# Hybrid decoder trunk on one core: weight tiles at another byte offset with each load, three buffers in place of four, two strips ahead

## The chip, the cores and the metric

The kernel runs on one core of a Trainium2 chip. The metric is the device time of one launch in microseconds (us). The times of before are three runs of the same program; the profile is of one more execution.

## What is computed

A batch of one, 512 tokens, 1024 channels. Two layers follow each other, each in a "macaron" form: half a SwiGLU feed-forward, a mixer, half a SwiGLU feed-forward. The first layer's mixer is an mLSTM in chunks; then one shared set of keys and values is made from the residual stream, and the second layer's mixer is a sparse attention over it (compressed blocks, selected blocks, a window). Cut to what matters here:

```python
D_MODEL, SEQ, D_FF = 1024, 512, 2816

def swiglu(h, w_in, w_out):
    a, b = jnp.split(h @ w_in, 2, axis=-1)
    return (jax.nn.silu(a) * b) @ w_out

x = x + 0.5 * swiglu(rmsnorm(x, g), w_in, w_out)    # ffn0
x = x + mlstm_mixer(rmsnorm(x, g), ...)             # mlstm
x = x + 0.5 * swiglu(rmsnorm(x, g), w_in, w_out)    # ffn1
...                                                 # kv: shared keys and values
x = x + 0.5 * swiglu(rmsnorm(x, g), w_in, w_out)    # ffn2
x = x + nsa_mixer(rmsnorm(x, g), ...)               # nsa
x = x + 0.5 * swiglu(rmsnorm(x, g), w_in, w_out)    # ffn3
```

All in float32. The four feed-forwards hold most of the multiplications.

## The kernel before

**Numbers.** Each float32 operand is split in two parts of the matmul's type: a high half (names ending in hi) and the low rest (lo). A product is three matmuls, hi·hi, hi·lo and lo·hi (`mm3`), issued by the helper at L234. The weights are the stationary operand, 128 x 128 at a time, and the activations the moving one: tiles of 128 channels by 512 tokens, or halves of them with 256 columns. Activations are named x (a feed-forward's normed input), t (sums of halves of x, 256 columns) and g (the gated hidden units).

**Stages.** In order of time: ffn0, mlstm, ffn1, kv, ffn2 (woven with the compression of keys and values), nsa, ffn3. ffn0, ffn1 and ffn3 (`SEVEN`) form their input products by a scheme with seven products in place of eight for a 2 x 2 split (`by_seven`); ffn2 does so from its second block on. The hidden units are worked through in blocks (`EVENS`: 0 to 8, 8 to 16 and 16 to 22, in units of 128; `LATER` in ffn2). A block is a row of by_seven units, one for a and one for b of each pair of hidden tiles, and then the block's share of the output product, `ffn_out`, eight strips with 512 columns.

**A unit** of `by_seven` has seven products of 12 matmuls with 256 columns (four channel tiles by three). VectorE takes the results out of PSUM between them: fq (L492) after the third product, fw (L495) and fu (L497) after the fourth, fw (L502) after the sixth, fu (L507) after the seventh. ScalarE copies the first (L487). A unit needs seven sums of weight quarters ("forms") in four groups, each in one pair of weight tiles: a11 and s1, s2 and s3, s4 and a12, and a22 alone. The quarters q come by DMA (`fetch`, L176), VectorE makes the sums s (`add_quarters`, L198 to L201), and `load_forms` splits each form: ScalarE writes the high half (L243), VectorE the low half as the difference (L244).

**Loads.** A "strip" in what follows is one such pair of tiles whi and wlo, 128 x 1024, from the pool "w" with four buffers. Other weights (ffn_out, the projections) come by `load_weight`: a DMA on SyncE's queue into wraw (two buffers), ScalarE writes whi (L171), VectorE wlo (L172). What is loaded when is set by a list: a dry pass records each `weight()` and `plan()` in the order that they are asked for, and in the real pass `weight()` issues entries of that list until 1 + `ahead` strips are ready, the one asked for among them. So the code of a load is issued `ahead` strips before its use, and stands at that place in the queues of SyncE, ScalarE and VectorE. Entries "fetch" and "add" stand in the list too and are issued with the strip behind them. `ahead` is 3 in ffn0, ffn1 and ffn3, 2 in ffn2 until its second block, then 3; from the fifth output strip of a feed-forward's last block on it is 2, as in the mixers. Within an engine, work runs in the order issued; a tile's next use waits until the last reader of the buffer is done.

```python
while self.order and len(self.ready) < 1 + self.ahead:
    self.load_weight()
key, w = self.ready.popleft()
```

**Places.** `STEP` and `placed` (L400 to L408) give the tiles t and g of ffn0, ffn1 and ffn3 64 words more than they need and start each at another multiple of 16 bytes in them (ffn3's t in steps of 4 words by a table of its own). x, the weights, and t and g of ffn2 start at the beginning of their tiles.

Of the kernel before, what the change touches and what calls it, by code (L numbers as in the profile page):

```python
# [11 lines left out]
F32R = mybir.dt.float32r  # L12
# [7 lines left out]
P = 128  # L20
# [58 lines left out]
class Steps:  # L79


    def __init__(self, gen):
        self.gen, self.may, self.due = gen, next(gen), 0.0
# [25 lines left out]
class Net:  # L109
    def __init__(self, ctx, tc, a, order=None):  # L110
        self.tc, self.nc, self.a, self.ctx = tc, tc.nc, a, ctx
        pool = lambda name, **k: ctx.enter_context(tc.tile_pool(name=name, **k))
        self.const = pool("const", bufs=1)
        self.hp = pool("h", bufs=1)
        self.wp = pool("w", bufs=4)
        self.xp = pool("x", bufs=8)
        self.sp = pool("stat", bufs=1)
        self.order = None if order is None else deque(order)
        self.asked = []
        self.ready = deque()  # L120
        self.raws, self.sums = {}, {}
        self.fp = None
        self.compressed = False
        self.ahead = 2


    def load_first(self):


        nc = self.nc  # L130
        name, idx = self.order.popleft()
        ap = self.a[name][idx]
        raw = self.wp.tile([P, 1024], F32, name="wraw", tag="wraw", bufs=2)
        hi = self.wp.tile([P, 1024], F32R, name="whi", tag="whi")
        lo = self.wp.tile([P, 1024], F32R, name="wlo", tag="wlo")
        v = lambda t: t.rearrange("p (n m) -> p n m", m=P)
        a, b = slice(0, 512), slice(512, 1024)
        for c, k in (a, slice(0, 4)), (b, slice(4, 8)):
            nc.scalar.dma_start(v(raw)[:, k], ap[:, k])
        nc.vector.tensor_copy(hi[:, a], raw[:, a])  # L140
        nc.vector.tensor_tensor(lo[:, a], raw[:, a], hi[:, a].bitcast(F32), op=ALU.subtract)
        self.ready.append(((name, idx), (v(hi), v(lo))))
        self.rest = lambda: self.split(raw[:, b], hi[:, b], lo[:, b])

    def load_weight(self):
        nc = self.nc
        name, idx = self.order.popleft()
        if name == "fetch":
            return self.fetch(*idx)
        if name == "add":  # L150
            return self.add_quarters(*idx)
        if name == "form":
            self.ready.append(((name, idx), self.load_forms(*idx)))
            return
        ap = self.a[name][idx] if idx else self.a[name]
        o = 1
        if len(ap.shape) == 4:
            p, o, n, m = ap.shape
        else:
            p, n, m = ap.shape  # L160
        w = o * n * m
        raw = self.wp.tile([P, 1024], F32, name="wraw", tag="wraw", bufs=2)
        if o == 1:
            nc.sync.dma_start(raw[:p, :w].rearrange("p (n m) -> p n m", m=m), ap)
        else:
            nc.sync.dma_start(raw[:p, :w].rearrange("p (o n m) -> p o n m", o=o, m=m), ap)
        hi = self.wp.tile([P, 1024], F32R, name="whi", tag="whi")
        lo = self.wp.tile([P, 1024], F32R, name="wlo", tag="wlo")

        for c in (slice(0, w // 2), slice(w // 2, w)) if name[0] in "mkc" else (slice(0, w),):  # L170
            nc.scalar.activation(hi[:p, c], raw[:p, c], AF.Copy)  # L171
            nc.vector.tensor_tensor(lo[:p, c], raw[:p, c], hi[:p, c].bitcast(F32), op=ALU.subtract)  # L172
        v = lambda t: t[:p, :w].rearrange("p (n m) -> p n m", m=m)
        self.ready.append(((name, idx), (v(hi), v(lo))))
# [28 lines left out]
    def load_forms(self, i, p, group):  # L203

        q, s = self.raws[i, p], self.sums[i, p]
        forms = ((q[1, 1], s[1]), (s[2], s[3]), (s[4], q[1, 2]), (q[2, 2],))[group]
        hi = self.wp.tile([P, 1024], F32R, name="whi", tag="whi")
        lo = self.wp.tile([P, 1024], F32R, name="wlo", tag="wlo")
        out = []
        for j, f in enumerate(forms):  # L210
            c = slice(512 * j, 512 * j + 512)
            self.split(f, hi[:, c], lo[:, c])
            out.append(tuple(t[:, c].rearrange("p (n m) -> p n m", m=P) for t in (hi, lo)))
        return out
# [159 lines left out]
    def ffn(self, i, given=None):  # L374

        nc, tc = self.nc, self.tc
        seven, r = i in SEVEN, None
        self.qbufs = 2 if seven else 1
        self.ahead = 3 if seven else 2
        TT, STT = nc.vector.tensor_tensor, nc.vector.scalar_tensor_tensor  # L380
        N = T // 2
        with ExitStack() as ctx:
# [4 lines left out]
            def room(name, words=96):  # L387

                nonlocal gp
                inner.close()  # L390
                gp = self.fp = inner.enter_context(tc.tile_pool(name=name, bufs=8, reuse_waits="tile"))

                nc.vector.memset(gp.tile([P, words], F32, name="home", tag="home", bufs=1)[:, :1], 0.0)
# [151 lines left out]
            for k0, k1 in EVENS if seven else LATER:  # L545
                gs, fold = [], seven and k1 < FB
                if not seven and k0 == LATER[1][0]:
                    brief.close()
                    room("fg2b", 32)
                    self.ahead = 3  # L550
                for p in range(k0, k1, 2) if seven or k0 else range(k0, k1):
                    if p and (seven or k0):
                        if p in units:
                            ts = [silu(t) for t in (yield from by_seven(p))]
                        else:
                            ts = []
                            for j in range(2):
                                w = self.weight("ffn_in", i, p + j)
# [903 lines left out]
```

## Time and profile before

| what | value |
|---|---|
| median of 3 runs | 1975.43 us (1973.61 to 1975.85) |
| profiled execution, its time | 1974.49 us |
| profiled execution, its span | 1972.7 us |
| matmuls, line L234, 256 columns on t | 3 x 1184 |
| matmuls, 256 columns on x | 3 x 888 |
| matmuls, 512 columns on g | 3 x 704 |
| matmuls, 512 columns on x | 3 x 480 |
| DMA, HBM read | 177.10 MB, 91 GB/s over the span |

The span is the time from the first to the last instruction of the profiled execution; the run's own time has 1.8 us more around it. PE is TensorE's matmuls, PEld its loading of weights, DVE VectorE, ACT ScalarE, SP SyncE, POOL GpSimd. Matmuls are pipelined: two neighbours overlap in the records, so a matmul's mean duration is longer than the distance from one start to the next, and a change of the one shows in the other. "<-" behind an idle time names what ended it. Times of a timeline count from the span's start. ffn0 runs until about 342 us, mlstm to 575, ffn1 to 912, kv to 1024, ffn2 to 1350, nsa to 1600, ffn3 to the end.

### The profile page before, as it was taken

What the parts mean: (1) busy time and instruction counts of PE and PEld (TensorE: products, weight loads), DVE (VectorE), ACT (ScalarE), POOL (GpSimd) and SP (SyncE); (2) the same over time, 40 slices, a digit from 0 to 9 for tenths busy, and PEclk for the clock granted to TensorE, in tenths of its full rate; (3) what the DMA queues carried; (4) which work ended last, traced back from release to release, by engine and by line L of the source; (5) the groups of instructions that cost most, each with busy time, mean ns of one, the idle gap of its engine ahead of it and who ended that gap; (6) DMA issues with size and microseconds to landing.
All of it is one profiled execution on the core that took longest, in us unless ns stands there. A gap on an engine that the chain in (4) does not pass through costs nothing.

```text
span 1972.7 us, 31765 instructions
## 1 busy us (share of the span) xinstructions
PE 1951.8 (99%) x11946; PEld 1724.3 (87%) x11946; DVE 1610.1 (82%) x3128; ACT 1014.6 (51%) x1912; POOL 167.4 (8%) x218
## 2 busy tenths in 40 slices
PE   9999999999999999999999999999999999999999
PEld 7989899788879999898788989898777879999897
DVE  8969879767888879698677979696788988879695
ACT  6525345455655435245354435354889965435242
POOL 0000000012200000000100000001444410000000
PEclk9999999999999999999999999999999999999999
DMA  5333422323232423323433333313232122323322
GB/s 190 109 100 102 117 77 74 111 86 97 65 118 86 118 85 98 106 72 105 114 121 119 114 111 97 104 63 116 74 88 65 54 97 86 118 82 101 106 72 91
DMA packets 81818, 192.80 MB, mean 98 GB/s; under 512 B 9856, under 2 KB 10752, under 8 KB 81664
## 3 DMA queue, kind: packets, MB, share of 16 engines
q1 hardware_dynamic: 80272, 188.02, 31.5%
q8 instruction: 94, 1.54, 0.3%
q0 software_dynamic: 384, 1.05, 0.3%
q10 hardware_dynamic: 1008, 1.70, 0.2%
q14 instruction: 60, 0.49, 0.1%
HBM read 177.10 MB, written 2.10 MB: 91 GB/s over the span
## 4 chain that ended last, share of the span: by engine, by line
PE 83%; DVE 8%; ACT 3%; DMA 2%; issue 1%; POOL 1%; SPq 0%; DVEq 0%; ACTq 0%; POOLq 0%
PE pmm L234 75%; PE vps L234 2%; PE S L234 1%; ACT pr L1202 1%; DVE wlo L172 1%; PE po L234 1%; DVE wlo L244 1%; DMA q<-in_ffn_in 1%; PE paux L234 1%; PE pt L1233 1%; DVE pr L1199 1%; PE pn L234 1%; ACT whi L171 1%; DVE ptl L244 0%; DMA wraw<-in_ffn_in 0%
## 5 line engine op out<-in xcount | busy, mean ns | idle before, releaser
L234 PE MATMUL pmm<-xhi,whi 128*128 128x256 f32 (+1 forms) x1376 | 444.2, 323 | 1.0 <-ACT whi L171 0.5
L234 PE MATMUL pmm<-xhi,wlo 128*128 128x256 f32 (+1 forms) x1376 | 442.5, 322 | 0.7 <-DVE wlo L172 0.7
L234 PE MATMUL pmm<-xlo,whi 128*128 128x256 f32 (+1 forms) x1376 | 442.2, 322 | 0.9 <-DVE xlo L288 0.8
L171 ACT ACTIVATE whi<-wraw 128x512 fp32r<-128x512 f32 (+3 forms) x258 | 203.9, 810 | 317.0 <-PE pmm L234 202.8
L234 PE MATMUL pmm<-thi,wlo 128*128 128x256 f32 x1184 | 333.0, 282 | 1.0 <-DVE wlo L244 1.0
L234 PE MATMUL pmm<-tlo,whi 128*128 128x256 f32 x1184 | 332.7, 281 | 0.0
L234 PE MATMUL pmm<-thi,whi 128*128 128x256 f32 x1184 | 332.4, 281 | 0.0
L234 PEld LDWEIGHTS pmm<-xhi,wlo 128*128 128x128 f32 x1376 | 260.5, 189 | 20.4 <-DVE wlo L172 1.1
L234 PEld LDWEIGHTS pmm<-xlo,whi 128*128 128x128 f32 x1376 | 260.6, 189 | 20.1 <-DVE xlo L288 2.7
L234 PE MATMUL pmm<-glo,whi 128*128 128x512 f32 x704 | 276.6, 393 | 0.8 <-DVE glo L244 0.8
L234 PEld LDWEIGHTS pmm<-xhi,whi 128*128 128x128 f32 x1376 | 260.3, 189 | 19.3 <-ACT whi L171 0.9
L234 PE MATMUL pmm<-ghi,wlo 128*128 128x512 f32 x704 | 276.8, 393 | 0.0
L234 PE MATMUL pmm<-ghi,whi 128*128 128x512 f32 x704 | 274.7, 393 | 0.0
L172 DVE TENSOR_TENSOR wlo<-wraw,whi 128x512 fp32r<-128x512 f32 (+3 forms) x258 | 237.9, 933 | 44.2 <-ACT whi L171 42.2
L243 ACT ACTIVATE whi<-s 128x512 fp32r<-128x512 f32 x222 | 139.5, 628 | 248.0 <-PE pmm L234 139.8
L234 PEld LDWEIGHTS pmm<-thi,wlo 128*128 128x128 f32 x1184 | 223.4, 189 | 1.2 <-DVE wlo L244 1.2
L234 PEld LDWEIGHTS pmm<-thi,whi 128*128 128x128 f32 x1184 | 223.8, 189 | 0.0
L234 PEld LDWEIGHTS pmm<-tlo,whi 128*128 128x128 f32 x1184 | 223.5, 189 | 0.0
L243 ACT ACTIVATE whi<-q 128x512 fp32r<-128x512 f32 x260 | 161.5, 624 | 115.6 <-PE pmm L234 103.8
L244 DVE TENSOR_TENSOR wlo<-q,whi 128x512 fp32r<-128x512 f32 x260 | 178.0, 685 | 15.9 <-ACT whi L243 15.8
L234 PEld LDWEIGHTS pmm<-glo,whi 128*128 128x128 f32 x704 | 132.4, 188 | 31.0 <-DVE glo L244 1.2
L234 PEld LDWEIGHTS pmm<-ghi,wlo 128*128 128x128 f32 x704 | 132.3, 188 | 30.2
(371 smaller groups left out, 3292.0 us busy)
## 6 DMA issues: line engine op xcount, KB each, us to landing
q<-in_ffn_in SPq DMA_DIRECT2D x260, 256.0 KB, 2.8
wraw<-in_ffn_out SPq DMA_DIRECT2D x48, 512.0 KB, 3.5
wraw<-in_ffn_out SPq DMA_DIRECT2D x48, 384.0 KB, 3.2
wraw<-in_ffn_in SPq DMA_DIRECT2D x27, 512.0 KB, 3.8
e<-in_ffn_in SPq DMA_DIRECT2D x36, 256.0 KB, 2.9
wraw<-in_m_qk SPq DMA_DIRECT2D x8, 512.0 KB, 3.7
wraw<-in_m_v SPq DMA_DIRECT2D x8, 512.0 KB, 3.7
wraw<-in_m_og SPq DMA_DIRECT2D x8, 512.0 KB, 3.7
```

The costliest lines, as they stand in the source:

```text
L171: nc.scalar.activation(hi[:p, c], raw[:p, c], AF.Copy)
L172: nc.vector.tensor_tensor(lo[:p, c], raw[:p, c], hi[:p, c].bitcast(F32), op=ALU.subtract)
L234: self.nc.tensor.matmul(out, lhsT, rhs, start=start, stop=stop)
L243: self.nc.scalar.activation(hi, src, AF.Copy)
L244: self.nc.vector.tensor_tensor(lo, src, hi.bitcast(F32), op=ALU.subtract)
L1199: nc.vector.tensor_tensor_reduce(s, S[:, i, :n], caus[:, T - n:], 1.0, -3e38, ALU.add, ALU.max, nx[:, i:i + 1])
L1202: nc.scalar.activation(s, s, AF.Exp, bias=nx[:, i:i + 1], scale=c[b][:, tb, j:j + 1], accum_out=z[:, i:i + 1])
L1233: nc.tensor.transpose(pt[:, col:col + P], pr[br][:, ROW[tb] + sb * P:ROW[tb] + sb * P + P], self.ident)
```

## The change

Weight tiles whi and wlo come from a new method `part`. It takes a tile of 1088 words in place of 1024 and returns 1024 of them, from word c on. c goes through all 16 multiples of 4 words (16 bytes) from 0 to 60, by another order for whi than for wlo, with a count of its own for each. The pool "w" has three buffers in place of four, and `ahead` is 2 everywhere.

```diff
-        self.wp = pool("w", bufs=4)
+        self.wp = pool("w", bufs=3)
...
+    def part(self, name):
+
+        k = self.places[name] = self.places.get(name, 0) + 1
+        c = 4 * ((5 * k + k // 16 if name == "whi" else 7 * k + 3 + k // 16) % 16)
+        return self.wp.tile([P, 1024 + 64], F32R, name=name, tag=name)[:, c:c + 1024]
...
-        hi = self.wp.tile([P, 1024], F32R, name="whi", tag="whi")
-        lo = self.wp.tile([P, 1024], F32R, name="wlo", tag="wlo")
+        hi = self.part("whi")
+        lo = self.part("wlo")
...
-        self.ahead = 3 if seven else 2
+        self.ahead = 2 if seven else 2
...
-                    self.ahead = 3
+                    self.ahead = 2
```

The pair of lines with `part` stands in `load_first`, `load_weight` and `load_forms`. From there on the changed kernel's lines are 7 higher: L244 is L251, L172 is L179, L492 is L499, L495 is L502, L497 is L504, L502 is L509, L507 is L514.

The shorter list ahead moves VectorE's work against itself. First a unit in the middle of ffn0's second block, on VectorE. fq, fw and fu are the unit's own results; s and q21 are the next unit's sums (q21 is written over with the third), and wlo the low halves of the next unit's forms. Before:

```order
L198 TENSOR_TENSOR s1_2098<-q21_1965,q22_1967 128x512
L244 TENSOR_TENSOR wlo_2114<-q11_1961,whi_2113 128x512
L199 TENSOR_TENSOR s2_2099<-s1_2098,q11_1961 128x512
L200 TENSOR_TENSOR q21_1965<-q11_1961,q21_1965 128x512
L201 TENSOR_TENSOR s4_2100<-q12_1963,s2_2099 128x512
L244 TENSOR_TENSOR wlo_2114<-s1_2098,whi_2113 128x512
L492 TENSOR_TENSOR fq_2067<-pmm_2062,fw_2066 128x256
L244 TENSOR_TENSOR wlo_2147<-s2_2099,whi_2146 128x512
L495 TENSOR_TENSOR fw_2066<-fq_2067,pmm_2063 128x512
L244 TENSOR_TENSOR wlo_2147<-q21_1965,whi_2146 128x512
L497 TENSOR_TENSOR fu_2068<-fw_2066,pmm_2063 128x256
L502 TENSOR_TENSOR fw_2066<-fw_2066,pmm_2064 128x512
```

And of the change, at the same unit:

```order
L499 TENSOR_TENSOR fq_2061<-pmm_2056,fw_2060 128x256
L205 TENSOR_TENSOR s1_2125<-q21_1992,q22_1994 128x512
L502 TENSOR_TENSOR fw_2060<-fq_2061,pmm_2057 128x512
L206 TENSOR_TENSOR s2_2126<-s1_2125,q11_1988 128x512
L504 TENSOR_TENSOR fu_2062<-fw_2060,pmm_2057 128x256
L207 TENSOR_TENSOR q21_1992<-q11_1988,q21_1992 128x512
L208 TENSOR_TENSOR s4_2127<-q12_1990,s2_2126 128x512
L251 TENSOR_TENSOR wlo_2141<-q11_1988,whi_2140 128x512
L251 TENSOR_TENSOR wlo_2141<-s1_2125,whi_2140 128x512
L509 TENSOR_TENSOR fw_2060<-fw_2060,pmm_2058 128x512
L251 TENSOR_TENSOR wlo_2172<-s2_2126,whi_2171 128x512
L251 TENSOR_TENSOR wlo_2172<-q21_1992,whi_2171 128x512
```

The next unit's four sums and its first pair of low halves (wlo_2114, now wlo_2141) stood ahead of the unit's first result, fq, and now stand behind it; the second pair (wlo_2147, now wlo_2172) stood around the result that follows the fourth product and now stands behind the one that follows the sixth (L509).

The second place is VectorE at the end of that block: the last unit's results, and the low halves of the first strips of ffn_out (L172, now L179, 1024 wide). Before:

```order
L172 TENSOR_TENSOR wlo_2532<-wraw_2529,whi_2531 128x1024
L199 TENSOR_TENSOR s2_2523<-s1_2522,q11_2389 128x512
L200 TENSOR_TENSOR q21_2393<-q11_2389,q21_2393 128x512
L201 TENSOR_TENSOR s4_2524<-q12_2391,s2_2523 128x512
L492 TENSOR_TENSOR fq_2491<-pmm_2486,fw_2490 128x256
L172 TENSOR_TENSOR wlo_2565<-wraw_2562,whi_2564 128x1024
L495 TENSOR_TENSOR fw_2490<-fq_2491,pmm_2487 128x512
```

And of the change:

```order
L499 TENSOR_TENSOR fq_2485<-pmm_2480,fw_2484 128x256
L205 TENSOR_TENSOR s1_2549<-q21_2420,q22_2422 128x512
L502 TENSOR_TENSOR fw_2484<-fq_2485,pmm_2481 128x512
L206 TENSOR_TENSOR s2_2550<-s1_2549,q11_2416 128x512
L504 TENSOR_TENSOR fu_2486<-fw_2484,pmm_2481 128x256
L207 TENSOR_TENSOR q21_2420<-q11_2416,q21_2420 128x512
L208 TENSOR_TENSOR s4_2551<-q12_2418,s2_2550 128x512
L179 TENSOR_TENSOR wlo_2559<-wraw_2556,whi_2558 128x1024
L509 TENSOR_TENSOR fw_2484<-fw_2484,pmm_2482 128x512
```

The first strip of ffn_out (wlo_2532, now wlo_2559) stood ahead of fq and now stands behind the result of the fourth product.

More of the change, by code (lines that the diff above doesn't have):

```diff
@@ L121, in __init__ @@
         self.raws, self.sums = {}, {}
+        self.places = {}
         self.fp = None
@@ L166, in load_weight @@
             nc.sync.dma_start(raw[:p, :w].rearrange("p (o n m) -> p o n m", o=o, m=m), ap)
-        hi = self.wp.tile([P, 1024], F32R, name="whi", tag="whi")
-        lo = self.wp.tile([P, 1024], F32R, name="wlo", tag="wlo")
+        hi = self.part("whi")
+        lo = self.part("wlo")
         for c in (slice(0, w // 2), slice(w // 2, w)) if name[0] in "mkc" else (slice(0, w),):
@@ L206, in load_forms @@
         forms = ((q[1, 1], s[1]), (s[2], s[3]), (s[4], q[1, 2]), (q[2, 2],))[group]
-        hi = self.wp.tile([P, 1024], F32R, name="whi", tag="whi")
-        lo = self.wp.tile([P, 1024], F32R, name="wlo", tag="wlo")
+        hi = self.part("whi")
+        lo = self.part("wlo")
         out = []
```

## The prediction

> **What bounds the kernel now.** First the page's own totals, then the longest unbroken pieces of the chain that ended last.
>
> ```profile
> span 1972.7 us, 31765 instructions
> PE 1951.8 (99%) x11946; PEld 1724.3 (87%) x11946; DVE 1610.1 (82%) x3128; ACT 1014.6 (51%) x1912; POOL 167.4 (8%) x218
> 38.22 319.74 PE pmm L234 x2155
> 1621.88 347.34 PE pmm L234 x2278
> ```
>
> TensorE is the bound, and in ffn0 (from 38.22 us) and ffn3 (from 1621.88 us) the chain of waits is one uninterrupted run of matmuls. Nothing is waited for there now, so the change can act in two ways only: the pitch of the matmuls may alter, or a wait may appear where there was none. What can be late is VectorE, and the table of windows shows how near it is.
>
> ```profile
> 140.00:150.00 10.00, 10.00 (x86) 10.00 (x85) 8.34 (x15) 4.37 (x9) 0.00 (x0) 1.00 0.18 60
> 187.00:207.00 20.00, 20.00 (x170) 20.00 (x170) 20.00 (x37) 11.06 (x20) 0.00 (x0) 1.00 0.34 106
> 208.00:218.00 10.00, 10.00 (x86) 10.00 (x85) 10.00 (x18) 6.42 (x10) 0.00 (x0) 1.00 0.34 102
> 310.00:320.00 10.00, 10.00 (x87) 10.00 (x86) 10.00 (x19) 4.84 (x9) 0.00 (x0) 1.00 0.01 2
> 1300.00:1310.00 10.00, 10.00 (x86) 10.00 (x85) 9.88 (x18) 5.80 (x11) 0.00 (x0) 1.00 0.39 124
> 1920.00:1930.00 10.00, 10.00 (x87) 10.00 (x86) 10.00 (x19) 5.72 (x10) 0.00 (x0) 1.00 0.00 0
> ```
>
> The columns are the stretch, its width, then busy time and count of PE, PEld, DVE, ACT, POOL, the granted clock, the DMA share and GB/s. At 140 us, the start of ffn0's second block, VectorE has slack (8.34 of 10). Towards the ends of blocks, in ffn0 and in ffn3, it has none (10.00 of 10). In ffn2 it has a little (9.88). ScalarE is half idle and the granted clock is 1.00 throughout, so neither enters the sum. The slack itself is the distance between the end of a low half (wlo) and the first matmul that reads it. The timeline shows it at a block's start, and at the first and the last of the nine block ends of ffn0, ffn1 and ffn3:
>
> ```profile
> 142.65 0.28 PE L234 MATMUL pmm<-thi,wlo 128*128 128x256 f32 x1
> 142.85 0.63 ACT L243 ACTIVATE whi<-q 128x512 fp32r<-128x512 f32 x1 [0.92 <-PE pmm L234]
> 144.12 0.69 DVE L244 TENSOR_TENSOR wlo<-s,whi 128x512 fp32r<-128x512 f32 x1
> 151.58 0.28 PE L234 MATMUL pmm<-thi,wlo 128*128 128x256 f32 x1
> 95.92 1.22 DVE L172 TENSOR_TENSOR wlo<-wraw,whi 128x1024 fp32r<-128x1024 f32 x1
> 98.17 0.39 PE L234 MATMUL pmm<-ghi,wlo 128*128 128x512 f32 x1
> 1925.49 0.69 DVE L244 TENSOR_TENSOR wlo<-s,whi 128x512 fp32r<-128x512 f32 x1
> 1927.14 0.28 PE L234 MATMUL pmm<-thi,wlo 128*128 128x256 f32 x1
> ```
>
> Each row is start, duration, engine and line. At the block's start a half is finished at 144.12 + 0.69 = 144.81 and first read at 151.58: 6.8 us of margin. At the first block's end it is 98.17 − (95.92 + 1.22) = 1.03 us, at the last 1927.14 − (1925.49 + 0.69) = 0.96 us. So run-ahead built while VectorE has little to do is spent by the end of each block, down to about 1 us. The second row gives the other half of the reading: ScalarE's copy into whi waited for PE, and started 0.2 us after a strip's last matmul (142.65). The conversion of a strip is held back by the buffer of the strip four earlier, so taking a buffer away moves it.
>
> **The change part by part.** *Three buffers, two strips ahead.* The high half of strip n can now begin when strip n−3 is read out, not n−4: one strip later.
>
> ```profile
> L234 PE MATMUL pmm<-thi,wlo 128*128 128x256 f32 x1184 | 333.0, 282 | 1.0 <-DVE wlo L244 1.0
> 146.98 0.69 DVE L244 TENSOR_TENSOR wlo<-s,whi 128x512 fp32r<-128x512 f32 x1
> 147.58 0.42 DVE L497 TENSOR_TENSOR fu<-fw,pmm 128x256 f32<-128x256 f32 x1
> 147.92 0.69 DVE L244 TENSOR_TENSOR wlo<-q,whi 128x512 fp32r<-128x512 f32 x1
> ```
>
> First the price of a unit. The two units from 187 to 207 us issue 170 matmuls in 20 us. A unit has seven products of 12 matmuls, 84, and its PE time is 84 × 20.00/170 = 9.9 us, call it 10.0; a product takes 1.43. For VectorE, a 512-wide operation costs 147.58 − 146.98 = 0.60 us back to back and a 256-wide one 0.34. Two units hold 32 of the first (14 forms, 8 sums, 4 results, 4 for the gates, 2 low halves of g) and 6 of the second: 19.2 + 2.0 = 21.2 us against 20.0. So VectorE loses about 0.6 us per unit, and run-ahead pays it.
>
> Now what run-ahead is lost. A strip of two products lasts 2.86 us, the one-product strip at a unit's end 1.43: on average (3 × 2.86 + 1.43)/4 = 2.5 us. Of these the margin at the block ends, about 1.0 us by the rows shown, is not needed now. That leaves 1.5 us a block end, and at nine ends 13 us. This is the *lower price*; with the shortest strip instead of the mean it would be 1.43 − 1.0 = 0.4, nine times 4 us.
>
> The *upper price* comes from the order of VectorE's queue, where the next unit's four sums and its group 0 now stand behind this unit's first result. That result waits for the third product, 3 × 1.43 = 4.3 us into the unit. Behind it follow a 256-wide operation, s1, the result L502, s2, the result L504 (256-wide), L207, L208 and the two halves of group 0: 7 × 0.60 + 2 × 0.34 = 4.9 us. The second half of group 0 is thus ready at 9.2 us into the unit; it is read in the next unit's second product, at 10.0 + 1.43 + 0.24 (its low half comes as the third matmul) = 11.7. The best margin that a unit can start with is 2.5 us instead of 6.8; 4.3 − 1.0 = 3.3 us a block end, 30 us in all. I take **20 us**, between the two: the 0.6 us of each unit comes off either margin in the same way, but some of the upper price is won back, since VectorE works on while PE waits. Both ends, 4 and 30, stay in the range.
>
> *What stands behind these waits.* The wait is PE's, on wlo; PE's queue is in order, so all later matmuls of the stage move by it. VectorE's next result (L492) in turn waits for those. Nothing of it returns later, because after each block PE has no idle time to give back. *ffn2* has two strips ahead in its first block before and after and loses the third one in its later blocks; VectorE has 0.1 us of slack in 10 there (9.88 at 1300 us) and more during ffn_out (18.64 of 30.00 at 1152 us, below), so run-ahead is hardly spent. I take 1 us there. In mlstm, kv and nsa PE waits for other things; the loads there were two ahead already and the third buffer covers them: nothing.
>
> *DMA.* Fetches and raw loads are issued by SyncE, and each is issued one strip later where a strip less is ahead. Landing is short beside a strip:
>
> ```profile
> q<-in_ffn_in SPq DMA_DIRECT2D x260, 256.0 KB, 2.8
> L198 DVE TENSOR_TENSOR s<-q,q 128x512 f32<-128x512 f32 x65 | 45.0, 692 | 4.7 <-DMA q<-in_ffn_in 3.0 <-DVE fq L492 1.7
> ```
>
> A fetch is issued at a unit's start, and its first sum now stands behind fq, 4.3 us later at the least; 2.8 us fit in. All the sums together waited 3.0 us for quarters; if the cover went they would wait some 2 us at a block's start, inside the range.
>
> *The byte offsets.* Today all weight tiles start at the same place modulo 256 bytes, and only t and g (in ffn0, 1 and 3) are spread. Does the distance between the two operands matter? The trace has both kinds:
>
> ```profile
> L234 PE MATMUL pmm<-tlo,whi 128*128 128x256 f32 x304 | 85.0, 280 | 0.0
> L234 PE MATMUL pmm<-xlo,whi 128*128 128x256 f32 x228 | 64.4, 282 | 0.0
> L234 PE MATMUL pmm<-ghi,wlo 128*128 128x512 f32 x145 | 57.3, 395 | 0.0
> L234 PE MATMUL pmm<-xhi,wlo 128*128 128x512 f32 x48 | 18.7, 390 | 0.0
> L234 PE MATMUL pmm<-ghi,whi 128*128 128x512 f32 x116 | 45.0, 389 | 0.0
> L234 PE MATMUL pmm<-xhi,wlo 128*128 128x512 f32 x480 | 188.5, 393 | 0.7 <-DVE wlo L172 0.7
> L234 PE MATMUL pmm<-xhi,wlo 128*128 128x256 f32 x888 | 250.9, 282 | 0.0
> 225.00:264.00 39.00, 39.00 (x170) 31.61 (x169) 22.71 (x32) 9.36 (x13) 0.00 (x0) 1.00 0.31 94
> 1152.00:1182.00 30.00, 30.00 (x134) 24.83 (x133) 18.64 (x28) 8.64 (x13) 0.00 (x0) 1.00 0.36 103
> ```
>
> The first four rows are ffn1's, the fifth ffn2's, then two of the whole run. With 256 columns the spread t is 2 ns shorter than the unspread x (280 against 282). With 512 columns it is the other way: spread g takes 395, unspread x 390 and ffn2's unspread g 389. The windows agree: ffn0's spread g has 39.00/170, about 0.229 us apart, ffn2's unspread g 30.00/134, 0.224, both a little too small by the matmuls cut at the borders. After the change every pair lies at another distance. The 512-wide ones that lose the equal place are ffn2's g (3 × 176 = 528) and x (3 × 480 = 1440, part of it in stages where PE waits anyway): between 0 and 5 ns, 0 to 9.8 us, and I take 5. The 256-wide x (3 × 888 = 2664) may gain the 2 ns: 0 to −5.3; where VectorE sets the pace the gain returns as waiting, and I take −2. Net **+3 us**, range −6 to +10.
>
> The Trainium skill, on the page "TensorE: Matmul & The Clock Gate", Part 2, "Step-by-step: what each phase is for", says that TensorE has two independent read ports into SBUF, so that loading the next weights takes nothing from the running matmul. By that rule the place of either operand is indifferent and this term would be 0 instead of 3. The trace does not agree: 389 against 395 ns for the same shape.
>
> **Sum.** The profiled execution took 1974.5 us (span 1972.7 and 1.8 around it); 20 + 1 + 3 make 1998.5. The median of the runs, 1975.4, is 0.9 above the profiled one: **1999 us**.
>
> **The rivals.** (A) *Two ahead is enough.* The waits stay away because VectorE starts each block with the same work done, and its loss per unit is smaller than I count. For it: the margin of 6.8 us at a block's start is larger than the strip lost. Against it: 1.0 at the end. Only the offsets are left: 1975 − 6 to 1975 + 10, likeliest 1978.
>
> (B) *The other side: the equal places cost more than they seem.* If each 256-wide matmul that now meets its weights at the same or a fixed distance ran 3 ns faster once the distance changes with every load, the 2664 of x and the 3552 of t would save 6216 × 3 ns = 19 us, giving 1956 if no wait appears. The point from which it decides is the waits: above 19 us of them nothing is left. For it: 280 against 282 ns. Against it: the row shows 2, not 3, and t is spread already.
>
> (C) *VectorE sets the pace in every unit.* If with one strip less no run-ahead builds at all, each of the 57 units of ffn0, 1 and 3 (19 each) takes VectorE's 10.6 us instead of 10.0 and starts no unit ahead: 57 × 0.6 = 34 us, with the 3 of the offsets and a few for idle time that the later buffers force on VectorE, 2016. For it: 10.00 of 10 at 187–218 us. Against it: 8.34 at 140 us.
>
> (D) *Place is indifferent*, as the rule quoted above has it. Then the offset term is 0 and the waits alone count: 1975.4 + 21 = 1996.
>
> **How the numbers follow.** The forecast gets 0.54, A 0.14, B 0.10, C 0.14, D 0.08. The likeliest is 1999. A measurement of this kernel can tell about 0.2%, 4 us, from no change. Faster by more than that are B and a fifth of A, 0.13; within it about half of A, 0.07; slower are the forecast, C, D and the rest of A, 0.80. The forecast's own range is 4 + 0 − 6 to 30 + 1 + 10 around 1975, that is 1973 to 2016. The range that should hold 8 in 10 leaves out B and the low half of A below, and the upper half of C above: **1975 to 2016**.
>
> **What would show it.** *Waits:* the unbroken pieces of 319.74 and 347.34 us break, with VectorE's wlo (L251, L179) between them, mostly in the second half of blocks; VectorE is at 10.00 of 10 there, and PE falls below it for the first time. If the pieces stay whole, A holds. *Order:* ScalarE's whi of group 0 starts about one strip later in the unit. *Offsets:* ffn2's g goes from 389 towards 395 ns, x with 256 columns from 282 towards 280, and the gap between the 512-wide kinds closes; equal means before and after speak for D, a fall of 3 ns or more for B. The forecast is wrong if PE waits for less than 4 us or more than 30 us in the three seven-product FFNs.

## The result, and the profile after

The change makes the kernel slower: 1994.01 us (1992.9 to 1994.51, 3 runs) against 1975.43 us, a ratio of 1.0095 with a 95% interval of 1.0072 to 1.0118. That is 18.6 us more; 23.6 more were forecast. The profiled execution has a span of 1992.2 us, 19.5 more than before, and a mean granted clock of 0.998.

The page of the changed kernel, and the longest pieces of its chain of waits (start, length, what ran) in ffn0 and ffn3, the two places shown of before:

```profile
span 1992.2 us, 31797 instructions
PE 1965.4 (99%) x11946; PEld 1725.5 (87%) x11946; DVE 1614.4 (81%) x3128; ACT 1013.2 (51%) x1912; POOL 167.1 (8%) x218
85.95 97.98 PE pmm L241 x642
212.02 103.39 PE pmm L241 x683
318.93 43.10 PE pmm L241 x224
...
1710.42 98.44 PE pmm L241 x642
1836.95 103.56 PE pmm L241 x683
1944.04 44.71 PE pmm L241 x224
```

The unbroken runs of 319.74 and 347.34 us are in pieces, and each cut lies near the end of a block: in ffn0 before 85.95, 212.02 and 318.93 us. The work is the same: in the row of the engines each has the count of instructions that it had before.

Where the time went by stage can be read from pieces of the chain that both kernels have. The first fence is before, the second after. Its first row stands 16 us behind ffn0, the second 28 us behind ffn1, the third 26 us behind ffn2, each already in the next stage.

```profile
357.97 5.55 PE pg L234 x24
...
939.66 5.61 PE pmm L234 x24
...
1375.80 5.60 PE pmm L234 x24
```

```profile
362.04 5.53 PE pg L241 x24
...
948.79 5.66 PE pmm L241 x24
...
1389.55 5.62 PE pmm L241 x24
```

The lag is 4.1 us behind ffn0, 9.1 behind ffn1, 13.8 behind ffn2 and 19.5 at the end: four to six in each feed-forward with its neighbours. What PE waited for is in the groups of its matmuls (the last columns are the idle time before them and what ended it). Two rows of the changed kernel:

```profile
L241 PE MATMUL pmm<-xhi,wlo 128*128 128x256 f32 x888 | 252.4, 284 | 12.8 <-DVE wlo L251 12.6
L241 PE MATMUL pmm<-thi,wlo 128*128 128x256 f32 x1184 | 333.8, 282 | 0.0
```

Of before these two were 0.0 and 1.0. So about 12 us are PE's waiting for low halves, all of it in products on x. The windows of the changed kernel show a second, smaller part around one of the longest of these waits, in ffn3's last block (the number ahead of the last two is the granted clock):

```profile
1936.00:1940.00 4.00, 4.00 (x35) 3.91 (x34) 4.00 (x9) 1.76 (x3) 0.00 (x0) 1.00 0.00 0
1940.00:1944.00 4.00, 2.05 (x18) 1.84 (x16) 4.00 (x9) 2.67 (x5) 0.00 (x0) 1.00 0.00 0
1944.00:1948.00 4.00, 3.96 (x23) 3.96 (x24) 4.00 (x8) 1.11 (x4) 0.00 (x0) 0.67 0.00 0
1948.00:1952.00 4.00, 4.00 (x33) 4.00 (x32) 2.18 (x5) 1.96 (x4) 0.00 (x0) 0.90 0.02 4
...
1112.00:1116.00 4.00, 3.62 (x17) 3.62 (x18) 3.94 (x7) 1.06 (x3) 0.00 (x0) 0.57 0.40 121
```

PE stands still for about 2 us (2.05 busy of 4), and right behind that its clock is down to 0.67 and 0.90: 4 x 0.33 + 4 x 0.10 = 1.7 us. The same happens once more, at the start of ffn2's second block (0.57, 1.7 us). Together 3.4 us that are no wait, but come behind waits. Before had a mean clock of 1.000.

This is what the wait itself looks like, in the timeline of the changed kernel:

```profile
1935.40 0.28 PE L241 MATMUL pmm<-thi,wlo 128*128 128x256 f32 x1
...
1939.63 0.42 DVE L499 TENSOR_TENSOR fq<-pmm,fw 128x256 f32<-128x256 f32 x1
...
1939.97 0.68 DVE L205 TENSOR_TENSOR s<-q,q 128x512 f32<-128x512 f32 x1
...
1940.57 0.68 DVE L502 TENSOR_TENSOR fw<-fq,pmm 128x512 f32<-128x512 f32 x1
...
1941.17 0.68 DVE L206 TENSOR_TENSOR s<-s,q 128x512 f32<-128x512 f32 x1
...
1941.77 0.41 DVE L504 TENSOR_TENSOR fu<-fw,pmm 128x256 f32<-128x256 f32 x1
1941.77 0.28 PE L241 MATMUL pmm<-tlo,whi 128*128 128x256 f32 x1
...
1942.10 0.69 DVE L207 TENSOR_TENSOR q<-q,q 128x512 f32<-128x512 f32 x1
...
1942.70 0.68 DVE L208 TENSOR_TENSOR s<-q,s 128x512 f32<-128x512 f32 x1
1943.30 0.69 DVE L251 TENSOR_TENSOR wlo<-q,whi 128x512 fp32r<-128x512 f32 x1
...
1943.90 0.68 DVE L251 TENSOR_TENSOR wlo<-s,whi 128x512 fp32r<-128x512 f32 x1
1944.04 0.39 PE L241 MATMUL pmm<-xhi,wlo 128*128 128x256 f32 x1 [1.99 <-DVE wlo L251]
```

VectorE works without a gap, through the very rows that the order shows, from fq to the next unit's first low halves. From fq's start to the end of the second half it takes 1944.58 - 1939.63 = 4.95 us; the prediction counted 4.9. But VectorE is late when it starts on fq. That operation needs the third product, whose last matmul is the row at 1935.40 (the 36 matmuls of products two to four are all in the timeline, and it is the 24th). It starts only at 1939.63, with no idle time of VectorE ahead of it: VectorE came from other work, 4 us late. PE issues its last matmul at 1941.77 and has to wait until 1944.04. It is let go by the first of the two halves, which ends at 1943.30 + 0.69 = 1943.99.

### The profile page after: what moved, and what is told of

It is laid out like the page before. It is cut to its first block, busy times and chain, and to the rows that moved or that the text cites. A ratio compares the mean times of both kernels' runs of the same rounds, so it can differ in the third digit from the quotient of the medians.

```text
span 1992.2 us, 31797 instructions
## 1 busy us (share of the span) xinstructions
PE 1965.4 (99%) x11946; PEld 1725.5 (87%) x11946; DVE 1614.4 (81%) x3128; ACT 1013.2 (51%) x1912; POOL 167.1 (8%) x218
## 4 chain that ended last, share of the span: by engine, by line
PE 80%; DVE 12%; ACT 4%; issue 2%; DMA 1%; POOL 0%; SPq 0%; DVEq 0%; ACTq 0%; POOLq 0%
PE pmm L241 73%; DVE wlo L251 3%; ACT pr L1209 2%; PE vps L241 1%; PE S L241 1%; PE paux L241 1%; PE po L241 1%; DVE wlo L179 1%; DVE pr L1206 1%; PE pt L1240 1%; PE pn L241 1%; DVE fw L502 1%; DVE s L208 1%; ACT pth L250 1%; DVE q L207 1%
## 5 line engine op out<-in xcount | busy, mean ns | idle before, releaser
L241 PE MATMUL pmm<-xhi,wlo 128*128 128x256 f32 (+1 forms) x1376 | 445.5, 324 | 13.3 <-DVE wlo L251 12.6
L179 DVE TENSOR_TENSOR wlo<-wraw,whi 128x512 fp32r<-128x512 f32 (+3 forms) x258 | 237.8, 935 | 44.8 <-ACT whi L178 43.1
L251 DVE TENSOR_TENSOR wlo<-q,whi 128x512 fp32r<-128x512 f32 x260 | 174.2, 685 | 9.1 <-ACT whi L250 9.1
```

The lines of the kernel that those rows point to most:

```text
L241: self.nc.tensor.matmul(out, lhsT, rhs, start=start, stop=stop)
L251: self.nc.vector.tensor_tensor(lo, src, hi.bitcast(F32), op=ALU.subtract)
```

## The experiments

**The two halves of the change.** First the buffers and the strips ahead without the offsets:

```diff
-        self.wp = pool("w", bufs=4)
+        self.wp = pool("w", bufs=3)
...
-        self.ahead = 3 if seven else 2
+        self.ahead = 2 if seven else 2
...
-                    self.ahead = 3
+                    self.ahead = 2
```

> Three buffers and two strips ahead, every weight tile at its old byte offset. If the change's loss is waits for low halves at the block ends (17 us of the 19 by the trace of after), this kernel is 13 to 19 us slower than before, about 1991 us, with PE waiting for wlo at the same places, and its pitch is that of before (512 columns on ffn2's g 389 ns, 256 columns on x 282). If the offsets brought the loss, it is within 3 us of before, about 1975.

Measured: 1990.36 us, 1.0084 of before (1.0071 to 1.0098), 16.1 us more than the 1974.22 of before in the same series. Then with the fourth buffer kept, `ahead` as above:

> Four buffers as before, but two strips ahead: VectorE's queue has the order of the change, and no load waits for a buffer longer than before. If the order in VectorE's queue costs (group 0 of the next unit behind fq), the waits stay: 10 to 17 us slower than before, about 1988, and the same as the kernel with three buffers within 4 us. If the late release of the third buffer costs, the waits go: 0 to 4 us slower than before, about 1977.

Measured: 1979.52 us, 1.0026 (1.0016 to 1.0035), 5.3 us more. Neither of the two clean cases came: the shorter list costs 5, taking the fourth buffer away 11 more. The row of PE's waits for low halves, first with three buffers, then with four:

```profile
L234 PE MATMUL pmm<-xhi,wlo 128*128 128x256 f32 x888 | 253.2, 285 | 12.7 <-DVE wlo L244 12.6
```

```profile
L234 PE MATMUL pmm<-xhi,wlo 128*128 128x256 f32 x888 | 251.7, 283 | 3.8 <-DVE wlo L244 3.7
```

With three buffers the waits are the changed kernel's 12.6 us to the tenth, so the offsets have no part in them. What the offsets cost is the distance to the changed kernel, 1994.0 - 1990.4 = 3.6 us, or 18.6 - 16.1 = 2.5 us if each is taken against before in its own series. In the middle of a block the order on VectorE is the same with three buffers and with four. So what the fourth buffer adds is taken to be how far conversion gets while VectorE has time to spare; no run shows that by itself.

**VectorE's pace.** Is it VectorE's work in a unit that eats the run-ahead? Two kernels take two of a unit's four sums away from it. One gives them to GpSimd:

```diff
-        TT(s[3], q[1, 1], q[2, 1], op=ALU.subtract)
-        TT(s[4], q[1, 2], s[2], op=ALU.subtract)
+        PT = self.nc.gpsimd.tensor_tensor
+        PT(s[3], q[1, 1], q[2, 1], op=ALU.subtract)
+        PT(s[4], q[1, 2], s[2], op=ALU.subtract)
```

> The change, with two of the four sums of each unit (the third and the fourth, 2 x 0.60 us) made by GpSimd in place of VectorE, so that VectorE has 9.4 us of work in a unit against 10.0 of PE. If run-ahead is spent because VectorE is slower than PE, the waits at the block ends (17 us) go nearly all: 1977 to 1983, that is 11 to 17 us faster than the change. If what counts is only the time from a buffer's release to the low half's end, independent of VectorE's load, the time stays: 1990 to 1996. If GpSimd's sums come late or slow VectorE down, it is slower than the change, above 1997.

Measured: 2034.02 us, 1.0298 (1.0284 to 1.0312), 40 us more than the changed kernel. The third case came, and it is no test of the pace, as the groups of instructions of this kernel show, beside the one of the changed kernel behind them:

```profile
L252 DVE TENSOR_TENSOR wlo<-s,whi 128x512 fp32r<-128x512 f32 x222 | 190.5, 859 | 0.0
L209 POOL TENSOR_TENSOR s<-q,s 128x512 f32<-128x512 f32 x65 | 99.0, 1523 | 317.8 <-ACT whi L251 163.7 <-issue 87.1 <-DVE wlo L252 56.7
```

```profile
L251 DVE TENSOR_TENSOR wlo<-s,whi 128x512 fp32r<-128x512 f32 x222 | 151.9, 685 | 0.0
```

A sum takes 1523 ns on GpSimd, and VectorE's low halves of sums, 685 ns in the changed kernel, take 859 on average in its presence. VectorE has two sums less in each unit, and is busy for 1612.4 us against 1614.4: the whole relief is given back, and the two sums take longer than before. The other kernel leaves the two sums out (the third form takes q21 as it is, the fourth sum is replaced by the second, so that these products are not the reference's):

```diff
-        TT(s[3], q[1, 1], q[2, 1], op=ALU.subtract)
-        TT(s[4], q[1, 2], s[2], op=ALU.subtract)
+        s[4] = s[2]
```

> The change, with the third and the fourth sum of each unit left out altogether (the quarter q21 stays as it is in its form, and the second sum stands in for the fourth), so that VectorE has 9.4 us of work in a unit against 10.0 of PE and GpSimd nothing. If the waits come from VectorE's being slower than PE, 14 or more of the 17 us go: 1977 to 1982, that is the offsets' 3 us and a little more above before. If they come from the time between a buffer's release and the low half's end, whatever VectorE's load, at most the 1.2 us of a unit's first group are saved at each stall, and the time is 1985 to 1992.

Measured: 1976.14 us, 1.0007 (0.9997 to 1.0017): the whole loss of the change is gone, with its three buffers, its shorter list and its offsets in place. That is 1.3 us (-0.6 to 3.4) above before, a little under the range that VectorE's pace was to give, and far from the other case, in which 1.2 us saved at each stall would still leave 0.8 of a wait of 2.0. PE's runs in ffn0 and ffn3 are whole again, and the waits on wlo are 0.3 us in the row that had 12.6 (0.9 in that of g):

```profile
35.71 320.94 PE pmm L240 x2165
...
1599.63 369.66 PE pmm L240 x2374
```

```profile
L240 PE MATMUL pmm<-xhi,wlo 128*128 128x256 f32 x888 | 249.4, 281 | 0.3 <-DVE wlo L250 0.3
```

From the other side, before with one sum made twice, four buffers and three ahead:

```diff
         TT(s[4], q[1, 2], s[2], op=ALU.subtract)
+        TT(s[4], q[1, 2], s[2], op=ALU.subtract)
```

> Before (four buffers, three ahead), with the fourth sum of each unit made twice, the same value: 0.60 us more of VectorE's work in a unit, 11.2 against 10.0 of PE. If run-ahead pays VectorE's excess until it is used up, the margin of about 1 us left at the block ends covers only the first of it: blocks of 5, 8 and 6 units lose 3.0 - 1, 4.8 - 1 and 3.6 - 1 us, 8.4 us in each of ffn0, ffn1 and ffn3, so 25 us in all: 1993 to 2003. If four buffers keep VectorE off PE's path whatever it does, or if the margins at the ends are no measure of it: 1975 to 1980.

Measured: 1982.87 us, 1.0046 (1.0029 to 1.0063), 8.6 us more, a third of the 25 expected. The direction is right, and waits for low halves appear (1.0 in this row of before):

```profile
L235 PE MATMUL pmm<-thi,wlo 128*128 128x256 f32 x1184 | 332.7, 282 | 4.6 <-DVE wlo L245 4.4
```

The sum over all units is not right. What fits the windows of before: at a block's start VectorE has time to spare (8.34 of 10 at 140 us) because the buffers are full, so work added there is free, and only the units behind that point draw on the run-ahead. That was not tried by itself.

**The order alone, at three buffers.** The changed kernel with the next unit's sums one strip earlier in the list:

```diff
-                a22 = self.weight("form", i, p, 3)[0]
                 upcoming("add", p)
+                a22 = self.weight("form", i, p, 3)[0]
```

> The change, with the next unit's sums put in the list one strip earlier, ahead of the unit's last group, so that they stand before the unit's first result on VectorE again; buffers as in the change. With four buffers the order alone cost 5 us and the third buffer 11 more. If the two add up, this gives back at most the 5: 1988 to 1992. If the third buffer costs only because the sums stand behind fq (the two together), most of the 16 goes: 1978 to 1984. If the sums' place costs nothing at three buffers: 1994.

Measured: 1987.02 us, 1.0063 (1.0050 to 1.0077), 7 us less than the changed kernel. That is 1 us below the range for two terms that add up, and far from the 16: the place of the sums behind fq is worth 6 to 7 of the 18.6 us (6 if each kernel is taken against before in its own series). In its timeline the sums stand ahead of fq again; the next unit's first low halves still stand behind it.

**Which half's buffers.** Three buffers, two ahead, the old offsets (the first kernel of this section), with four buffers for one half alone:

```diff
-        hi = self.wp.tile([P, 1024], F32R, name="whi", tag="whi")
+        hi = self.wp.tile([P, 1024], F32R, name="whi", tag="whi", bufs=4)
```

> Three buffers, two ahead and the old offsets, but four buffers for the high halves alone. If the third buffer costs because ScalarE's copy starts late, the 11 us between three and four buffers go: 1978 to 1982. If it costs because VectorE's own write into wlo waits for the release, only ScalarE's 0.6 us at each strip are saved: 1985 to 1990.

```diff
-        lo = self.wp.tile([P, 1024], F32R, name="wlo", tag="wlo")
+        lo = self.wp.tile([P, 1024], F32R, name="wlo", tag="wlo", bufs=4)
```

> The other half of that pair: four buffers for the low halves alone, three for the high ones. A low half cannot start before its high half, so with ScalarE's late start as the cause nothing is saved: 1988 to 1992. If the release of wlo is the cause: 1978 to 1982.

Measured: 2005.64 us with four for whi (1.0161, 1.0146 to 1.0176) and 1993.38 with four for wlo (1.0096, 1.0081 to 1.0111), against 1990.36 with three for both. The second is near what ScalarE's late start would give, the first fits neither theory: a fourth buffer for the high halves alone saves nothing and costs 15 us. So only the two together give the 11 us. In PE's row of waits for low halves (12.6 us with three of both) both kernels have 10.5, and at the block ends of ffn0, ffn1 and ffn3 the waits are the same as with three of both, up to 2.0 us each. Some of the 15 is the clock: the mean granted clock is 0.996 in that execution against 0.999 with three of both, 0.003 x 2000 = 6 us. Another piece is a wait of 2.8 us at 1645 us, where ffn3 begins, for an operation of ScalarE (sq). Why four buffers for whi bring these, and what the rest is, stays open.

**The offsets by themselves.** With four buffers there is no room for tiles of 1088 words, so the high halves got 4 words more each: four buffers, four distances to x.

```diff
-        hi = self.wp.tile([P, 1024], F32R, name="whi", tag="whi")
+        hi = self.wp.tile([P, 1028], F32R, name="whi", tag="whi")[:, :1024]
...
-                    room("fg2b", 32)
+                    room("fg2b", 1)
```

> Four buffers, three ahead, the old order; only the high halves whi are moved, each buffer by one step more than the one before it, so that x lies 32, 64, 96 or 128 bytes from them by turns and the same as before from wlo. If the distance of the two operands sets the pitch as the traces of before and after read (plus 5 ns with 512 columns, minus 0.6 with 256), two thirds of the 512-wide x and of ffn2's g get 5 ns longer and two thirds of the 256-wide x 0.6 ns shorter: 3 to 7 us slower, about 1980, and hi-hi products change while hi-lo products don't. If place is indifferent: 1975, within 2 us. If varied places save 3 ns each with 256 columns: 8 to 12 us faster, about 1965.

Measured: 1976.45 us, 1.0010 (1.0001 to 1.0019), 2.2 us more: the sign as by the traces, a little below the 3 expected. One part of the expectation failed: with 512 columns the products of x with wlo, which was to keep its distance, went from 393 to 396 ns too, like those with whi. Neighbours overlap in the records, so a mean does not tell the two apart. And with one constant distance of 64 bytes:

```diff
         self.sp = pool("stat", bufs=1)
+        tc.nc.vector.memset(self.xp.tile([P, 16], F32, name="pad", tag="pad", bufs=1), 0.0)
```

> Before, with x and everything allocated behind it 64 bytes further on; weights stay, and each distance between the operands is another one, but the same with each load. If an equal place is what the 512-wide matmuls gain from, the 512-wide x and ffn2's g go from 389 or 390 towards 394 ns and 256-wide x from 282 to 281: 4 to 9 us slower, about 1982. If only the variation from load to load matters, or nothing of it: 1975, within 2 us.

Measured: 1973.88 us, 0.9998 (0.9989 to 1.0007): no change. The time fits "only variation matters", the groups don't. Of this kernel:

```profile
L235 PE MATMUL pmm<-xlo,whi 128*128 128x256 f32 x888 | 248.0, 279 | 0.0
...
L235 PE MATMUL pmm<-xlo,whi 128*128 128x512 f32 x480 | 189.2, 394 | 0.5 <-DVE xlo L289 0.5
```

Of before these were 282 and 393 ns. The constant distance makes the 256-wide matmuls 3 ns shorter and the 512-wide ones 1 longer, and the sum is nothing. So a constant distance matters too, and not only one that changes with each load.

**A faster kernel.** If the equal place is good with 512 columns, g of ffn0, ffn1 and ffn3 should have it:

```diff
-                    c = (STEP[kind][i][part](k) - 128) % 256 // 4
+                    c = (STEP[kind][i][part](k) - 128) % 256 // 4 if kind == "t" else 0
```

> Before, with g of ffn0, ffn1 and ffn3 at the beginning of its tile, so that all 512-wide matmuls lie at the weights' own place modulo 256 bytes. If the equal place is worth the 5 ns that ffn2's g shows, 1584 matmuls save 8 us: 1965 to 1969. If the 5 ns are ffn2's own (other buffers, less of VectorE beside it): 1974, within 2 us.

Measured: 1965.69 us, 0.9956 (0.9942 to 0.9970): 8.6 us faster than before, and faster than the change by 28. Its row of g, then that of before:

```profile
L234 PE MATMUL pmm<-ghi,wlo 128*128 128x512 f32 x704 | 273.8, 389 | 0.0
```

```profile
L234 PE MATMUL pmm<-ghi,wlo 128*128 128x512 f32 x704 | 276.8, 393 | 0.0
```

Both together, g at the equal place (word 48 in its tile) and x 64 bytes off:

> g of ffn0, ffn1 and ffn3 at the weights' place as in the kernel with g alone, and x and ffn2's g 64 bytes off as in the kernel with the constant shift (which measured no change: 256-wide x 1.8 ns shorter, 512-wide ones 1 to 2 longer). If places add up matmul by matmul, the gain is g's alone: 1965 to 1969, within 2 us of that kernel. If the two meet in some other way: outside of that.

Measured: 1966.03 us, 0.9957 (0.9945 to 0.9970), the same as with g alone.

## Why the prediction was right, point by point

**What bounds it.** Right: PE's unbroken runs of ffn0 and ffn3 broke at the block ends, and VectorE was what they waited for. That VectorE's pace drains the run-ahead is shown from both sides, by the kernel with two sums less (no loss) and the one with a sum more (8.6 us). Late quarters have no part in it: VectorE's s1 sums (L198, now L205) waited 4.7 us in all before and 0.9 after. The prediction's remark that landing is short beside a strip was wrong, 2.8 us against 2.86, but nothing came of it.

**The waits.** 20 us were taken for the three seven-product feed-forwards and 1 for ffn2, 21 in all, between a lower price of 13 and an upper one of 30. Buffers and list without the offsets measured 16.1 us in all. Of the changed kernel's 12.6 us of waits 2.1 are ffn2's and 10.5 the other three's: half of the 20, and a little under the lower price. Nor are the nine block ends alike. By the timeline they have 0.4, 1.4 and 2.0 us in ffn0, and 0, about 1.4 and 2.0 in ffn1 and in ffn3.

Three steps of the upper price were wrong. It took each unit's 0.6 us off the margin from the block's first unit on; the kernel with one sum more lost a third of what that counting gives. It took the order on VectorE to be the whole matter; the order alone, with four buffers, costs 5.3 us, and the buffer 10.8 more. And it read the margin, 2.5 us, at the second half of group 0. The first half is ready one operation earlier, at 8.6 us, but it is read one product earlier, at 10.0 + 0.24 = 10.2, which leaves 1.6. By the timeline it is this half that PE waits for at every block end: the 12.6 us stand in the row of x, and the row of t, which reads the second half, has 0.0. By that the upper price would have been higher still, and further off.

The step "the shortest strip, 4 us" was too small. The lower price, a strip's run-ahead less what was left over at the block ends, came nearest, though only as a mean over unlike block ends. That the total came within 5 us is luck in part: the 20 was a choice between two prices, and some of what it had too much was made up for by the clock and by ffn2, which the sum did not have.

**ffn2.** Mis-sized: 1 us was taken. There the changed kernel's PE waits 2.06 us for one low half, against 0.97 for this unit's second form before, and has one of the two clock drops (1.7 us): 2.8 us. The place is not the later blocks' run-ahead that the prediction looked at, but the start of the second block. The timelines of before and, behind it, of the changed kernel show the low half of the first unit's first form (e is a quarter in a tile of its own, as q elsewhere), and the changed kernel's first use of it:

```profile
1095.84 0.68 DVE L244 TENSOR_TENSOR wlo<-e,whi 128x512 fp32r<-128x512 f32 x1
...
1097.77 0.96 DVE L244 TENSOR_TENSOR tlo<-tv,thi 128x768 fp32r<-128x768 f32 x1 [0.91 <-ACT thi L243]
...
1099.98 0.68 DVE L200 TENSOR_TENSOR e<-e,e 128x512 f32<-128x512 f32 x1
```

```profile
1109.57 0.69 DVE L207 TENSOR_TENSOR e<-e,e 128x512 f32<-128x512 f32 x1
1110.17 0.95 DVE L251 TENSOR_TENSOR tlo<-tv,thi 128x768 fp32r<-128x768 f32 x1
...
1111.64 0.69 DVE L251 TENSOR_TENSOR wlo<-e,whi 128x512 fp32r<-128x512 f32 x1
...
1112.38 0.47 PE L241 MATMUL pmm<-xhi,wlo 128*128 128x256 f32 x1 [2.06 <-DVE wlo L251]
```

Before, that low half stood ahead of t's last low half and of the unit's sums; now it stands behind both, and PE waits 2.06 us for it.

**The clock.** Not foreseen. The prediction took the granted clock of 1.00 as given; 3.4 of the 19.5 us between the two profiled executions are a lower clock behind two of the waits. With the waits, 11.6 (12.6 less the 1.0 of before), that makes 15.0. The other 4.5 were not taken apart, and the pieces do not simply add up: PE's whole idle time, span less busy time, grew only from 20.9 to 26.8 us, since waits for other things became shorter, while its busy time grew by 13.6.

**The offsets.** Right in sign, and in size as far as it is known: +3 was taken. The distance between the changed kernel and the one without them is 3.6 us, or 2.5 if each is taken against before in its own series. The kernel with two sums less, which has the same offsets and no waits to speak of, is only 1.3 us above before. The rows of ffn1 in the changed kernel answer to those shown of before (280, 282, 395 and 390 ns):

```profile
L241 PE MATMUL pmm<-tlo,whi 128*128 128x256 f32 x304 | 85.3, 280 | 0.0
L241 PE MATMUL pmm<-xlo,whi 128*128 128x256 f32 x228 | 63.9, 281 | 0.0
L241 PE MATMUL pmm<-ghi,wlo 128*128 128x512 f32 x145 | 57.4, 396 | 0.0
L241 PE MATMUL pmm<-xhi,wlo 128*128 128x512 f32 x48 | 18.9, 395 | 0.0
```

The 512-wide x went from 390 to 395, as foreseen, and the 256-wide x gained 1 ns where 2 were allowed. The page "TensorE: Matmul & The Clock Gate" of the Trainium skill, Part 2, "Step-by-step: what each phase is for", has the two operands read through ports of their own, which was taken as a rival in which place is indifferent. The kernel with g at the equal place speaks against place being indifferent: 4 ns of 393 and 8.6 us by place alone.

**The rivals.** A (two ahead is enough) fell: 16.1 us of waits and what follows them. B (varied places save 3 ns with 256 columns) fell for the change's offsets, 1 ns here; a constant distance of 64 bytes did give the 3 ns, and lost them again with 512 columns. C (VectorE sets the pace in every unit) fell: the pieces of about 100 us between the waits are unbroken, and the loss is half of its price. D fell by the rows of g; by the time alone its 1996 would have been nearer than the 1999, since the waits were taken too large.

## What to carry to other kernels

Where a slower helper engine is carried by run-ahead that builds up at one place and is spent at another, the margin at the end of the spending tells more of what a buffer is worth than the mean load of the engine (13 us by that margin, 10.5 of waits and 16.1 of time here); read it as the time from a tile's last write to its first use at the last unit of each block. A loss that one strip less brings can also be taken away by a little less work of that engine in each unit (1.2 of 10.6 us did it here). Byte offsets between the moving and the stationary operand are worth trying for each width apart, since what helped 256 columns here (64 bytes) hurt 512.

## What the runs showed that was not expected

Waits of only 2 us came ahead of a lower clock, and not always: of the three waits of 2.0 us in the last blocks of ffn0, ffn1 and ffn3 of the changed kernel, the last was followed by a clock of 0.67 in the 4 us behind it and the first two were not, and in the kernel with three buffers and the old offsets it was that of ffn1 (0.77 and 0.80 in two windows of 4 us), while its wait of 2.45 us in ffn2 was followed by none. So two profiles of one loss can differ by 1.7 us for each such stretch alone.

```profile
896.00:900.00 4.00, 2.12 (x11) 2.12 (x12) 4.00 (x8) 2.00 (x4) 0.00 (x0) 0.77 0.00 0
900.00:904.00 4.00, 4.00 (x30) 4.00 (x30) 3.92 (x8) 2.06 (x4) 0.00 (x0) 0.80 0.00 0
```

GpSimd beside VectorE made VectorE's low halves of sums a quarter longer on average (685 to 859 ns) and those of quarters a seventh (685 to 783), on top of taking 1523 ns for what VectorE does in 685.
